# Operands of a gate made beside another block's out product, stored operands split later, attention outputs stored later

## The chip, the cores and the metric

The kernel runs on one core of a Trainium2 chip. A core has five engines with an instruction queue each: TensorE (PE, matrix products, with its weight loads shown apart as PEld), VectorE (DVE), ScalarE (ACT), GpSimd (POOL) and SyncE (SP). In this kernel SP does nothing but issue DMAs, and all DMAs are issued there, in the order of its queue: an issue that must wait (for a buffer, or for the data to be stored) holds back every issue behind it. The metric is the device time of one execution in microseconds; the time of a version is the median of its runs.

## The reference

One layer of a streaming encoder on 2048 prompt frames and 32 sample frames, in single precision, width 1024:

```
a  = rmsnorm(h) @ w_in                         # one projection, split into q, k, v of two groups
oa = differential attention                    # group A: 4 heads, two softmaxes each, v of 128
ob = chunk-band attention                      # group B: 8 heads of 64, a band of 9 chunks of 64
h  = h + concat(rmsnorm(oa), rmsnorm(ob)) @ w_out
c  = rmsnorm(h)
h  = h + square(relu(c @ w_up)) @ w_down       # 1024 -> 4096 -> 1024
h  = h + sigmoid(h @ w_ple_gate) * (p @ w_ple_proj)
y  = rmsnorm(h)
```

Beside `y` the new keys and values of both groups are outputs. Everything runs for the prompt and for the sample frames, which also see a cache of 128 older frames.

## The kernel before, in words

**Tiling.** The frames lie in four blocks: three of 512, and block 3 of 544 (512 prompt frames and the 32 sample frames). Activations are kept transposed, features on the 128 partitions, as eight tiles of 128 features. Every large product is made of three matmuls (`mm3`, lines 216 to 218): each operand is split into a rounded part and a rest (`split`: a copy on ACT, line 181, and a subtraction on POOL, lines 166 and 176, or on DVE, line 187), and high x high, high x low and low x high are summed in PSUM. Weights are loaded raw (`wr`, 512 KB each) and split in two halves (`piece`) by `wunit`; the pieces form a ring of a few units, which a unit leaves when TensorE has read it.

**Stages.** First the projections with the short attention (`attn_a` with `small`), then band attention, then the long attention of group A (`attn_a` for pairs 4 to 8) interleaved with the out products and MLPs of blocks 0 and 1, then block 1's gate. After that comes the part that most of the change touches, in `run`, lines 1595 to 1640:

- block 2's out product (`outproj(2)`), with the loading of block 3's attention outputs;
- block 3's out product, `outproj(3)`: eight groups `d` of 48 matmuls, which add to the residual (`hd`), square it on ACT and sum the squares on POOL (`sqacc`). Beside its last five groups runs `cparts(2)` in four steps `k`: each loads two tiles of block 2's residual (`tmp<-hS`), normalizes them (line 1011), and forms and splits the seven operands of block 2's MLP (`cs`; subtractions at lines 1023 to 1026);
- `h` of block 0 is loaded whole (2 MB, `h<-hS`) into memory that `outproj(3)`'s operands held, and `gate(0)` splits it into `hu` (eight ACT copies, four subtractions on DVE, four on POOL) and multiplies: eight groups of 24 matmuls `gps<-hu` and 6 of `pps<-pT`, a sigmoid on ACT, and an add into `h` on POOL (line 1361). Beside it, block 2's MLP makes its first weights;
- `mlp7(2)`: block 2's MLP, sixteen chunks, each with seven half-size up products (`ups`) and eight groups of down products (`dps`). Beside it run `final(0)`, four steps that write `y`, and `cstage(3)`, which prepares block 3's MLP operands as `cparts` does, but stores them to DRAM (`cst`, from rows `ct`) in eight steps: per `k` a step with two loads and three splits, and a step with four subtractions and four splits. Each split is stored at once;
- block 2's gate, block 3's MLP (which loads the stored operands into `cs`), and block 3's gate and final.

**Order.** The functions are generators; `weave` takes a step of one after each step of another, which sets the order of allocation and of priority. The framework then orders each engine's instructions by a simulated timeline and picks the buffers of the rings, and each engine runs its instructions strictly in that order. `tc.issue_after(x)` places an instruction behind `x`.

**Attention outputs.** `attn_a_pair` (line 591) handles a pair of 128-frame tiles of one head: scores, two softmaxes, transposes, value products over chunks of four key tiles (`v`, loaded chunk by chunk, two buffers), and a norm whose last instruction on DVE writes `os` (line 733). The store `oT<-os` is issued right there. `os` has two buffers.

## Time and profile before

| | us |
|---|---|
| median of 3 runs | 3171.91 (3171.86 to 3174.97) |
| the profiled execution | 3169.83 |
| its span, first to last instruction | 3168.0 |
| TensorE busy | 3014.8 (95%) |
| VectorE, ScalarE, GpSimd busy | 1900.8, 1880.1, 1837.4 |
| mean granted TensorE clock | 0.981 |

Times in the rows count from the start of the span. A group or timeline row names the line of the kernel, the engine, the operation, the tile written and the tiles read; brackets show how long the engine had been idle before and what ended that. A row of the waits names the waiting engine, line and tile, then what it waited for, the total in us, how often, and the longest. A row of the windows gives a stretch, its length, the busy time of PE, PEld, DVE, ACT and POOL (instructions in brackets), the granted clock (1.00 is full), the share of the DMA engines and GB/s. In a row of one tile's instructions the three numbers behind the count are the shortest, median and longest duration in ns, then the first and last start. Lines of helpers (166, 176, 181, 187, 216 to 218, 157 for every DMA) are told apart by their tiles.

### The profile page before, as it was taken

What the parts mean: (1) busy time and instruction counts of PE and PEld (TensorE: products, weight loads), DVE (VectorE), ACT (ScalarE), POOL (GpSimd) and SP (SyncE); (2) the same over time, 40 slices, a digit from 0 to 9 for tenths busy, and PEclk for the clock granted to TensorE, in tenths of its full rate; (3) what the DMA queues carried; (4) which work ended last, traced back from release to release, by engine and by line L of the source; (5) the groups of instructions that cost most, each with busy time, mean ns of one, the idle gap of its engine ahead of it and who ended that gap; (6) DMA issues with size and microseconds to landing.
All of it is one profiled execution on the core that took longest, in us unless ns stands there. A gap on an engine that the chain in (4) does not pass through costs nothing. (4 is left out here: it accounts for less than half of the span.)

```text
span 3168.0 us, 52770 instructions
## 1 busy us (share of the span) xinstructions
PE 3014.8 (95%) x17913; PEld 2656.2 (84%) x17913; DVE 1900.8 (60%) x4596; ACT 1880.1 (59%) x4166; POOL 1837.4 (58%) x2496
## 2 busy tenths in 40 slices
PE   8999898999999999999999999999799999999998
PEld 7787787899877787878788788878688888999998
DVE  5158774655465654676756656435667885576653
ACT  6257775766676664766666657444555455554545
POOL 2447455332346544655655555677777778767674
PEclk9999999999999999999999999999899999999999
DMA  8788758986788645555563543537433446333231
GB/s 274 247 243 245 205 185 233 262 229 194 219 243 245 194 125 151 154 148 153 171 182 117 143 116 108 169 106 234 134 120 120 157 134 228 122 105 110 87 115 56
DMA packets 522134, 537.17 MB, mean 170 GB/s; under 512 B 38620, under 2 KB 401440, under 8 KB 521864
## 3 DMA queue, kind: packets, MB, share of 16 engines
q1 hardware_dynamic: 521864, 533.80, 56.6%
q8 instruction: 142, 2.33, 0.3%
q14 instruction: 128, 1.05, 0.1%
HBM read 419.88 MB, written 117.75 MB: 170 GB/s over the span
## 5 line engine op out<-in xcount | busy, mean ns | idle before, releaser
L176 POOL TENSOR_TENSOR wl<-wr,wh 128x256 fp32r<-128x256 f32 x648 | 473.2, 763 | 351.6 <-ACT wh L181 321.6
L181 ACT ACTIVATE piece<-wr 128x512 fp32r<-128x512 f32 x406 | 246.4, 625 | 283.9 <-PE ups L217 108.5
L176 POOL TENSOR_TENSOR piece<-wr,piece 128x256 fp32r<-128x256 f32 x404 | 326.1, 834 | 103.2 <-ACT piece L181 93.8
L181 ACT ACTIVATE wh<-wr 128x1024 fp32r<-128x1024 f32 x228 | 241.0, 1058 | 184.6 <-PE qps L217 42.1
L166 POOL TENSOR_TENSOR wl<-wr,wh 128x256 fp32r<-128x256 f32 x264 | 199.0, 786 | 199.7 <-ACT wh L181 193.4
L218 PE MATMUL dps<-uh,piece 128*128 128x272 f32 (+1 forms) x768 | 248.1, 325 | 6.0 <-POOL piece L166 5.9
L216 PE MATMUL dps<-uh,piece 128*128 128x272 f32 (+1 forms) x768 | 247.0, 325 | 5.0 <-ACT piece L181 2.1
L166 POOL TENSOR_TENSOR piece<-wr,piece 128x256 fp32r<-128x256 f32 x280 | 232.5, 862 | 27.1 <-ACT piece L181 22.8
L217 PE MATMUL dps<-ul,piece 128*128 128x272 f32 (+1 forms) x768 | 248.0, 324 | 0.0
L216 PE MATMUL ups<-cs,piece 128*128 128x256 f32 (+1 forms) x864 | 246.7, 286 | 1.0 <-DVE r L1219 1.0
L217 PE MATMUL ups<-cs,piece 128*128 128x256 f32 (+1 forms) x864 | 245.9, 285 | 0.0
L218 PE MATMUL ups<-cs,piece 128*128 128x256 f32 (+1 forms) x864 | 245.9, 285 | 0.0
L216 PE MATMUL qps<-aH,wh 128*128 128x512 f32 (+1 forms) x640 | 231.5, 362 | 9.1 <-ACT kn L506 4.5
L218 PE MATMUL qps<-aH,wl 128*128 128x512 f32 (+1 forms) x640 | 229.8, 359 | 0.0
L217 PE MATMUL qps<-aL,wh 128*128 128x512 f32 (+1 forms) x640 | 229.0, 358 | 0.0
L1160 DVE TENSOR_TENSOR h<-h,dps 128x512 f32<-128x512 f32 x256 | 174.6, 682 | 80.6 <-PE dps L218 75.0
L1208 DVE TENSOR_TENSOR h<-h,dps 128x272 f32<-128x272 f32 (+1 forms) x384 | 189.5, 514 | 54.8 <-PE dps L218 53.9
L216 PE MATMUL dps<-uh,wh 128*128 128x512 f32 x512 | 209.5, 409 | 12.5 <-DVE h L1160 6.1
L216 PE MATMUL ups<-cH,wh 128*128 128x512 f32 x512 | 203.0, 397 | 5.5 <-DMA kbt<-kS 5.1
L633 PE MATMUL s<-ka,q 128*128 128x512 f32 (+3 forms) x768 | 187.8, 345 | 17.5 <-ACT e L647 7.0
L218 PE MATMUL dps<-uh,wl 128*128 128x512 f32 x512 | 203.1, 397 | 0.5 <-POOL wl L166 0.4
L217 PE MATMUL dps<-ul,wh 128*128 128x512 f32 x512 | 202.3, 395 | 0.0
(314 smaller groups left out, 9636.9 us busy)
## 6 DMA issues: line engine op xcount, KB each, us to landing
wr<-w_up SPq DMA_DIRECT2D x128, 512.0 KB, 3.9
wr<-w_down SPq DMA_DIRECT2D x128, 512.0 KB, 3.8
wr<-w_in SPq DMA_DIRECT2D x74, 512.0 KB, 5.4
q<-qS SPq DMA_DIRECT2D x128, 256.0 KB, 5.1
v<-vSa SPq DMA_DIRECT2D x64, 512.0 KB, 3.8
ka<-kS SPq DMA_DIRECT2D x32, 512.0 KB, 9.3
wr<-w_out SPq DMA_DIRECT2D x32, 512.0 KB, 4.4
wr<-w_ple_gate SPq DMA_DIRECT2D x32, 512.0 KB, 4.3
```

The lines of the kernel that those rows point to most:

```text
L166: nc.gpsimd.tensor_tensor(out[:, sl], a[:, sl], b[:, sl], op=op)
L176: nc.gpsimd.tensor_tensor(out[:, sl], a[:, sl], b[:, sl], op=op)
L181: nc.scalar.activation(hi, raw, AF.Copy)
L216: nc.tensor.matmul(ps, lh, rh, start=start and i == 0, stop=False)
L217: nc.tensor.matmul(ps, lh, rl, start=False, stop=False)
L218: nc.tensor.matmul(ps, ll, rh, start=False, stop=stop and i == n - 1)
L633: nc.tensor.matmul(s, q[:, m, hl, P * qi : P * qi + nr], kt[:, m, k0 - kb : k0 - kb + n], start=hl == 0, stop=hl == 1)
L1160: nc.vector.tensor_tensor(hv, hv, ps, op=ALU.add)
L1208: nc.vector.tensor_tensor(hv, hv, ps, op=ALU.add)
```

## The change

Three edits. (1) A new generator, `hparts`, loads block 0's residual in eight tiles (`hraw<-hS`, 256 KB each) and splits them into `hu`; its three steps are taken after the first three groups of `outproj(3)`. `gate(0)` gets these operands (`made`) and splits nothing; it still loads `h` for the add. `cparts(2)` takes two of its four steps beside `outproj(3)` and the other two beside `gate(0)`, ahead of the first weights of block 2's MLP. (2) `cstage`: the four splits that follow the subtractions are issued after the next `k`'s rows are loaded and normalized, and the three splits of a `k` one step after its rows; nine steps in place of eight. (3) In `attn_a_pair` the store of `os` is kept in `late`, and issued behind the load of the third chunk of `v` of the next pair, or at the latest at the end of the next pair; with `small` it is issued at once, as before.

```diff
@@ attn_a, attn_a_pair
+        late = []
...
-                self.attn_a_pair(g, j if j < 8 else None, kt if j < 8 else ks, ba, pool, ps_s, ps_t, ps_o)
+                self.attn_a_pair(g, j if j < 8 else None, kt if j < 8 else ks, ba, pool, ps_s, ps_t, ps_o, late)
+                if self.small:
+                    late.pop(0)()
+        while late:
+            late.pop(0)()
...
-                self.dma(
+                ins = self.dma(
                     v[:, :nch].rearrange("p k a b -> p k (a b)"),
...
+                if c0 == 8 and late:
+                    with self.tc.issue_after(ins.ins):
+                        late.pop(0)()
...
-        self.dma(self.oT[:, g, t0 : t0 + nq], os_)
+        while late:
+            late.pop(0)()
+        late.append(lambda: self.dma(self.oT[:, g, t0 : t0 + nq], os_))
@@ cstage
+        def parts(k, *which):
+            for x, raw in which:
+                t = up.tile([P, up.aw], F32R, tag="u", name="cst")[:, :n]
+                self.split(t[:, :m], t[:, m:], raw, "act", "dve")
+                self.dma(out[x][:, :, k], t.rearrange("p (i c) -> p i c", i=2))
+
+        late = ()
         for k in range(4):
...
+            parts(k - 1, *late)
+            yield
             (b11, b12), (b21, b22) = c
...
-            parts(("b11", "dve"), ("b21", "dve"), ("b22", "dve"))
-            yield
+            parts(k, ("b11", b11), ("b21", b21), ("b22", b22))
             nc.vector.tensor_tensor(b22, b22, b12, op=ALU.subtract)
...
-            parts(("t2", "dve"), ("t1", "dve"), ("t3", "dve"), ("t4", "dve"))
+            late = (("t2", b11), ("t1", b12), ("t3", b22), ("t4", b21))
             yield
+        parts(3, *late)
+        yield
@@ hparts, gate
+    def hparts(self, b, wk, up, out):
+        n, t0 = BN[b], 512 * b
+        hH, hL = [[up.tile([P, BLK], F32R, tag="u", name="hu")[:, :n] for k in range(8)] for _ in range(2)]
+        out.append((hH, hL))
+        for k in range(8):
+            raw = wk.tile([P, BLK], F32, tag="tmp", bufs=self.nt, name="hraw")[:, :n]
+            self.dma(raw, self.hS[:, k, t0 : t0 + n])
+            self.split(hH[k], hL[k], raw, "act", "dve" if k % 2 else "pool")
+            if k in (2, 5):
+                yield
...
-        for k in range(8):
-            self.split(hH[k], hL[k], h[:, k, :n], "act", "dve" if k % 2 else "pool")
+        if made is None:
+            for k in range(8):
+                self.split(hH[k], hL[k], h[:, k, :n], "act", "dve" if k % 2 else "pool")
@@ run
                 g = self.outproj(3, wk, oa[3], md, acc[3])
+                made = []
+                hp = self.hparts(0, wk, up, made)
                 for _ in range(3):
                     next(g)
+                    next(hp, None)
                 r2 = self.colnorm(acc[2][0], 2, 1.0 / D, wk, mm, "mm", None)
-                weave(g, self.cparts(2, wk, cs, ops, r2), 1)
+                c = self.cparts(2, wk, cs, ops, r2)
+                weave(g, islice(c, 2), 1)
...
-            g = self.gate(0, h, up, None, md, wk)
+            g = self.gate(0, h, up, None, md, wk, made[0])
...
-            weave(g, self.along(iter(range(3)), m), 1)
+            weave(g, self.along(c, m), 1)
```

More of the change, by code (lines that the diff above doesn't have):

```diff
@@ L2 @@
 from contextlib import ExitStack
-from itertools import chain
+from itertools import chain, islice
 import numpy as np
@@ L1045, in cstage @@
                 c.append((tmp[:, :m], tmp[:, m:]))
+            parts(k - 1, *late)
+            yield
             (b11, b12), (b21, b22) = c
-            raw = {"b11": b11, "b21": b21, "b22": b22, "t3": b22, "t1": b12, "t2": b11, "t4": b21}
-            def parts(*which):
-                for x, e in which:
-                    t = up.tile([P, up.aw], F32R, tag="u", name="cst")[:, :n]
-                    self.split(t[:, :m], t[:, m:], raw[x], "act", e)
-                    self.dma(out[x][:, :, k], t.rearrange("p (i c) -> p i c", i=2))
-            parts(("b11", "dve"), ("b21", "dve"), ("b22", "dve"))
-            yield
+            parts(k, ("b11", b11), ("b21", b21), ("b22", b22))
             nc.vector.tensor_tensor(b22, b22, b12, op=ALU.subtract)
@@ L1301, in gfin, with gate @@
         self.dma(self.gf, self.a["g_final"].unsqueeze(0).broadcast_to([P, D]))
[L1303 removed]
+    def hparts(self, b, wk, up, out):
[8 more added lines that the diff above has]
+                yield
+    def gate(self, b, h, up, act, md, wk=None, made=None):
         nc, a = self.nc, self.a
@@ L1310, in gate @@
                 self.dma(pT[i][k][:, :n], self.pS[:, i, k, t0 : t0 + n])
-        if wk is None and act.aw is None:
+        if made is not None:
+            hH, hL = made
+        elif wk is None and act.aw is None:
             hc = [act.tile([P, 4, 272], F32R, tag="cs", name="hc").rearrange("p a b -> p (a b)") for _ in range(8)]
```

5 lines of the change are left out of this document (2 added, 3 removed).

## The prediction

> **What bounds the kernel now.** First the page: TensorE is busy for 95% of the span, so only its idle time and its slow stretches can be won. Then the chain of waits of PE, longest first, and the busy time by stretch (columns: PE, weight load, DVE, ACT, POOL, then granted clock, DMA share, GB/s).
>
> ```profile
> span 3168.0 us, 52770 instructions
> PE 3014.8 (95%) x17913; PEld 2656.2 (84%) x17913; DVE 1900.8 (60%) x4596; ACT 1880.1 (59%) x4166; POOL 1837.4 (58%) x2496
> ...
> GB/s 274 247 243 245 205 185 233 262 229 194 219 243 245 194 125 151 154 148 153 171 182 117 143 116 108 169 106 234 134 120 120 157 134 228 122 105 110 87 115 56
> ...
> PE gps L216 <- ACT hu L181: 20.2, 1, 20.2
> PE o L719 <- ACT pH L712: 7.4, 4, 3.7
> ...
> 2180.00:2228.00 48.00, 48.00 (x383) 47.91 (x382) 24.74 (x38) 19.57 (x39) 38.15 (x49) 1.00 0.72 215
> 2228.00:2249.00 21.00, 0.76 (x7) 0.54 (x5) 20.17 (x32) 10.62 (x25) 15.40 (x19) 0.63 0.76 259
> 2249.00:2290.00 41.00, 41.00 (x167) 33.02 (x168) 14.88 (x18) 21.53 (x38) 32.96 (x42) 0.94 0.18 52
> ...
> 2450.00:2620.00 170.00, 164.39 (x1017) 145.56 (x1016) 137.38 (x209) 89.90 (x175) 134.72 (x151) 1.00 0.46 150
> 2740.00:3090.00 350.00, 349.01 (x2782) 348.69 (x2781) 239.45 (x480) 175.74 (x320) 250.68 (x316) 1.00 0.32 103
> ```
>
> One wait stands far above the rest: at the start of block 0's gate TensorE is idle for 20.2 us, waiting for `hu`, the gate's operands. In those 21 us VectorE is busy for 20.17: it is the bound there, and for nobody but the gate. The timeline shows why.
>
> ```profile
> 2228.36 0.28 PE L218 MATMUL ops<-oact,piece 128*128 128x272 f32 x1
> 2248.89 0.80 PE L216 MATMUL gps<-hu,piece 128*128 128x512 f32 x1 [20.24 <-ACT hu L181]
> ...
> 2253.75 0.45 PE L216 MATMUL pps<-pT,piece 128*128 128x512 f32 x1
> 2254.03 0.39 PE L217 MATMUL pps<-pT,piece 128*128 128x512 f32 x1
> ...
> 2256.12 0.39 PE L217 MATMUL gps<-hu,piece 128*128 128x512 f32 x1
> ...
> 2229.74 0.74 DVE L1011 SCALAR_TENSOR_TENSOR tmp<-tmp,g_mlp_s,r 128x512 f32<-128x512 f32 x1
> ...
> 2238.50 0.74 DVE L1011 SCALAR_TENSOR_TENSOR tmp<-tmp,g_mlp_s,r 128x512 f32<-128x512 f32 x1
> ...
> 2247.24 0.41 DVE L187 TENSOR_TENSOR cs<-tmp,cs 128x256 fp32r<-128x256 f32 x1
> ...
> 2248.22 4.26 ACT L181 ACTIVATE hu<-h 128x512 fp32r<-128x512 f32 x8
> ...
> 2235.99 0.57 SPq L157 DMA_DIRECT2D h<-hS  x1
> ```
>
> Block 3's out product ends at 2228.4. VectorE is then still in the last two of `cparts`' four steps: one starts at 2229.74, the next at 2238.50 (8.76 us a step), the last subtraction at 2247.24. ACT's `hu` copies stand behind them in ACT's order and start at 2248.22. After the idle time the first eleven matmuls, 2248.89 to 2253.75, are 4.86/11 = 0.442 us apart; from 2254.03 to 2256.12 nine steps take 0.232 each. So the stall costs 20.24 + 11 x (0.442 - 0.232) = 20.2 + 2.3 = 22.5 us. That is by far the largest single item of this trace.
>
> **The change, part by part.** *Gate operands earlier.* Eight loads `hraw` (256 KB each) and eight splits are issued with the first three groups of block 3's out product; `cparts` keeps two steps there, and its other two go beside the gate. In the changed program's order all eight ACT copies stand ahead of `cparts`' first one, so nothing of the late chain holds the gate. Gone: 20.2 + 2.3 us. What was added, and its cover:
>
> - DMA: 2 MB of `hraw`, and 1 MB of `pT` that was loaded before block 2's out product, in 48 us that moved 215 GB/s x 48 = 10.3 MB. Without the two `tmp` loads that leave this stretch (0.5 MB), 12.8 MB is 267 GB/s; the page's fastest slice moved 274. The share was 0.72, so I cost it at nothing; without that cover it would be 2.5 MB at 259 GB/s, 10 us, on weight loads that run several groups of 6 us ahead.
> - SP: eight issues more; `h<-hS` is still loaded (the residual add needs it) but only after the out product's last matmul, in whose memory it lies. Behind it on SP stand `w_up` twice, `cparts`' last four loads and three gate weights. The first reader of `h` is POOL's add of the gate's first group, with 19 POOL instructions ahead of it in the gate; the load takes 10.1 us (the landing row below).
> - ACT and DVE: the splits are moved, not added: 4.3 us of ACT, and of DVE the same four subtractions. Two steps of `cparts`, 17.5 us of DVE, go into a gate in which DVE was busy for 14.88 of 41: covered. They are due when block 2's MLP starts, 55.7 us after the gate does.
> - POOL is the engine to watch. The gate is 8 groups x 30 matmuls x 0.232 = 55.7 us of PE.
>
> ```profile
> L176 POOL TENSOR_TENSOR piece<-wr,piece 128x256 fp32r<-128x256 f32 x60 | 47.8, 824 | 10.7 <-ACT piece L181 10.3
> ...
> L166 POOL TENSOR_TENSOR hu<-h,hu 128x256 fp32r<-128x256 f32 x8 | 7.5, 971 | 0.3 <-ACT hu L181 0.3
> ...
> L166 POOL TENSOR_TENSOR hu<-h,hu x8: 736/1008/1181, 2248.9 to 2255.7; 128x256 fp32r<-128x256 f32 x8
> ...
> DMA to landing us min/median/max: 10.1/10.1/10.1
> ```
>
> In the out product POOL has 48 - 38.15 = 9.9 us free; `hu` takes 7.5 (8 x 0.971). From the gate's second weight on, POOL's order holds 59 instructions up to the last gate weight, and 39 up to the second half of the fifth group's. At 0.824 each that is 48.6 and 32.1 us from about 2228. The fifth group's half is due 4 x 6.96 us plus 14 matmuls, 31.1 us, after 2228.4; the last one 52.0 us after. So POOL is 0.6 us late at the fifth group and in time at the end: I take 1.0 us of new stall. The ends: none at 0.736 each; at 1.181 each 59 take 69.7 us, 17.3 too many. I take 0.824 because its row is of these very instructions, sixty of them in this stretch.
>
> The Trainium skill, "SBUF — State Buffer", section "SBUF: two separate sides", speaks against packing more of DVE beside POOL: it says that a two-input DVE operation and a POOL operation exclude each other on a shared port pair for a whole instruction. The spread from 736 to 1181 ns of one POOL form, the long ones beside DVE's own `hu` subtractions, agrees with it. By that rule alone the stall would be up to 17 us in place of 1; it is the first rival.
>
> *Stored operands split a chunk later (`cstage`).* Loads, splits and stores keep their number; the splits that follow a row load are issued one step later, so that no store waits at the head of SP for a load that has just been issued. There is one step more, nine instead of eight; with `final`'s four that makes 13 in a loop of 14.
>
> ```profile
> PE dps L218 <- POOL piece L166: 3.9, 6, 1.0
> PE dps L216 <- ACT piece L181: 1.5, 2, 1.1
> ...
> SPq L157 <- DVE cst L187: 10.9, 13, 1.7
> ...
> L187 DVE TENSOR_TENSOR cst<-ct,cst x28: 427/974/984, 2460.0 to 2615.5; 128x272 fp32r<-128x272 f32 x28
> ...
> L216 PE MATMUL gps<-hu,piece x128: 388/396/795, 2248.9 to 2720.7; 128*128 128x512 f32 x128
> ```
>
> While `cstage` runs (2450 to 2620) PE waits 5.4 us in eight waits, all for weights of the down product; SP waits 10.9 us for `cst`, and `w_down` stands behind it. At most 5.4 us can go. The third MLP runs a like loop without `cstage` for 350 us with 1.0 us of PE idle, but there each chunk has more PE time to hide in. I take 1.5 us, since most of the waits are for POOL, whose work does not change. The other end: the last stores come one chunk later (84 matmuls of half width and 48 of full width, 90 x 0.232 = 21 us), some 2637 in place of 2616, and what they hold is first read behind block 2's gate, whose last group is at 2720.7. So a loss has no room but in reordering; 1 us, the longest single wait here.
>
> *Attention outputs stored a pair later.* In the long attention stage (1120 to 2060) each `oT<-os` goes behind the third value load of the next pair; the short stage keeps its order. A pair's buffer is one of two and is wanted again two pairs on, so a store one pair late holds nobody. First the waits of that stage (SP, PE, ACT), then the two PE waits that follow a late load.
>
> ```profile
> SPq L157 <- DVE os L733: 54.1, 14, 11.8
> ...
> PE s L633 <- DMA q<-qS: 4.0, 4, 1.7
> ...
> ACT wh L181 <- DMA wr<-w_down: 29.4, 6, 9.0
> ...
> 1646.00 0.70 PE L633 MATMUL s<-ka,q 128*128 128x512 f32 x2 [0.87 <-DMA q<-qS]
> ...
> 1770.80 1.06 ACT L181 ACTIVATE wh<-wr 128x1024 fp32r<-128x1024 f32 x1 [7.50 <-DMA wr<-w_down]
> ...
> 1773.81 0.50 PE L216 MATMUL dps<-uh,wh 128*128 128x512 f32 x1 [2.98 <-ACT relu L1125]
> ```
>
> SP loses 54.1 us at the head of its queue, but PE waits for a load it delays only 4.0 us. Most of SP's time then goes to the next wait in line, a raw weight buffer. I take half of 4.0: 2.0 us. The ends: 4.0 + 2.98 = 7.0 gained; lost, 2.98 at one place if a burst of key loads that now starts earlier pushes a weight load back.
>
> *The sum* against the profiled execution's own 3169.83 us: - 20.2 - 2.3 + 1.0 - 1.5 - 2.0 = - 25.0, that is 3144.8. The median of the three runs shown is 3171.91, 2.1 above the profiled one; so 3147 for the median.
>
> **The rivals.**
> 1. *POOL becomes the bound in the gate.* DVE is busier beside it, each POOL instruction takes the 1.18 us that `hu` shows, and 17.3 us of the stall come back as waits for weights. For it: POOL had 32.96 of 41 us in the gate. Against: sixty like instructions took 0.824. 3171.9 - 22.5 + 17.3 - 3.5 = 3163.
> 2. *The stores free more than PE's waits show.* The whole 7.0 us and all 5.4 of `cstage`: 3171.9 - 22.5 - 12.4 = 3137. Against: few PE waits follow SP's.
> 3. *Slower: the stores' new place makes a weight load late at every pair.* Loads that no longer wait behind a store go out in one burst with the keys, and each of the 20 stores moved costs the 2.98 us that the late `w_down` at 1773.81 cost: 60 us, 3171.9 - 25 + 60 = 3207. It decides from nine pairs on (9 x 2.98 = 26.8). Against: ACT waited for a `w_down` six times in 940 us, 29.4 us together, and TensorE felt little of it.
> 4. *The change doesn't do what it says*: the `hu` splits land late and the gate waits as before, 3170. Against: they are issued with the first three of eight groups of 6 us (48 us in all), 30 us before they are due.
>
> **How the numbers follow.** Forecast 0.63 (3141 to 3153 by itself); rival 1 0.15; rival 2 0.10; rival 3 0.06; rival 4 0.06. The range 3136 to 3163 leaves out rivals 3 and 4 and the far ends of rivals 1 and 2. 0.2% is 6.3 us, about what a measurement of this kernel can tell: faster is the forecast, rival 2 and nearly all of rival 1, 0.87; same is rival 4 and the rest of rival 1, 0.07; slower is rival 3, 0.06.
>
> **What would show it.** In the profile after: no wait of `gps` for `hu`, granted clock near 1.00 where it was 0.63; `hu` splits of `hraw` before `cparts`; gate waits for POOL's pieces of about 1 us (17 says rival 1); waits for `cst` gone from SP and PE's waits in block 2's MLP below 5.4; `DVE os` gone from SP's waits in the long attention and `q<-qS` below 4.0. It is wrong if block 2's MLP starts with a wait for `cs`, or if ACT waits for `w_down` more often than in six places.

## The result, and the profile after

| | before | after |
|---|---|---|
| median of five executions (us) | 3171.91 (3169.77 to 3175.32) | 3156.93 (3146.42 to 3159.81) |
| ratio, 95% interval | | 0.9941, 0.9928 to 0.9954 |
| the profiled execution, its span | 3169.83, 3168.0 | 3146.42, 3144.6 |

The change makes the kernel 15 us faster by the medians, and 18.7 us (14.6 to 22.8) by the ratio, which is formed from all executions; 25 us, to 3147, was predicted. The measured median lies inside the stated range of 3136 to 3163, but 10 us above the forecast and only 6 us below the price of rival 1. The profiled execution of the changed kernel is the fastest of its five, so the two traces stand 23.4 us apart, and only a part of that is the change. The page of the changed kernel, and its waits of PE over the whole span (longest first, rows between left out):

```profile
span 3144.6 us, 52811 instructions
PE 3011.4 (96%) x17913; PEld 2649.6 (84%) x17913; DVE 1897.6 (60%) x4596; ACT 1878.1 (60%) x4166; POOL 1847.6 (59%) x2496
```

```profile
PE o L727 <- ACT pH L720: 7.8, 4, 3.7
...
PE gps L216 <- ACT piece L181: 6.5, 1, 6.5
...
PE s L638 <- DMA q<-qS: 3.6, 4, 1.6
```

The 20.2 us wait of `gps` for `hu` is gone. In its place stands a new wait of 6.5 us of the same product for a `piece`, a split gate weight. The busy time by stretch (PE, weight load, DVE, ACT, POOL, clock, DMA share, GB/s) for the last 48 us of block 3's out product, for the 21 us that were the stall, for 41 us of gate, and for `cstage` (here 175 us long), each shifted by what the changed kernel is ahead:

```profile
2170.00:2218.00 48.00, 48.00 (x381) 47.76 (x380) 21.34 (x33) 21.06 (x40) 40.17 (x51) 1.00 0.81 260
2218.00:2239.00 21.00, 19.55 (x85) 15.71 (x85) 12.33 (x20) 10.36 (x22) 19.00 (x24) 1.00 0.68 222
2239.00:2280.00 41.00, 32.87 (x132) 25.49 (x132) 31.34 (x42) 27.89 (x55) 37.24 (x43) 0.92 0.36 116
2425.00:2600.00 175.00, 172.10 (x1065) 152.55 (x1064) 145.10 (x219) 91.38 (x177) 144.41 (x158) 1.00 0.47 150
```

The out product carries the added loads and splits without losing anything (PE 48.00 of 48). The former stall is filled (19.55 of 21, full clock). But 8 us are lost in the gate behind it: TensorE is busy for 32.87 of 41 us where it was busy for all 41.00, at a clock of 0.92. The timeline of that place, PE, then SP, DVE and ACT:

```profile
2219.70 0.47 PE L216 MATMUL gps<-hu,piece 128*128 128x512 f32 x1 [1.45 <-DVE hd L980]
...
2250.24 0.50 PE L218 MATMUL gps<-hu,piece 128*128 128x512 f32 x1 [1.60 <-POOL piece L176]
...
2259.30 0.80 PE L216 MATMUL gps<-hu,piece 128*128 128x512 f32 x1 [6.46 <-ACT piece L181]
...
2233.63 8.29 SPq L157 DMA_DIRECT2D wr<-w_up  x2
2241.97 0.97 SPq L157 DMA_DIRECT2D tmp<-hS  x2
2246.69 0.38 SPq L157 DMA_DIRECT2D wr<-w_ple_gate  x1
2247.12 1.05 SPq L157 DMA_DIRECT2D tmp<-hS  x2
...
2246.58 0.74 DVE L1021 SCALAR_TENSOR_TENSOR tmp<-tmp,g_mlp_s,r 128x512 f32<-128x512 f32 x1
...
2254.58 0.42 ACT L181 ACTIVATE cs<-tmp 128x256 fp32r<-128x256 f32 x1 [1.41 <-DVE tmp L1033]
...
2258.31 0.42 ACT L181 ACTIVATE cs<-tmp 128x256 fp32r<-128x256 f32 x1 [1.31 <-DVE tmp L1035]
2258.63 0.62 ACT L181 ACTIVATE piece<-wr 128x512 fp32r<-128x512 f32 x1
```

The gate starts at 2219.70 after a wait of 1.45 us for the add (`hd`) of the out product's sixth group. Its fifth group stops twice, 1.60 us for POOL's half of a weight and 6.46 us for the second half on ACT, split at 2258.63, 38.9 us after the gate began. In front of that split ACT's order holds the `cs` copies of the two steps of `cparts` that the change moved here, and they wait for DVE. DVE begins the first of these steps at 2246.58. Its rows (`tmp<-hS`) were issued only at 2241.97, behind two `w_up` loads that held SP's queue for 8.29 us, and the first of them landed at 2245.95; in DVE's own order the step also stands behind work on the second `w_up`, for which DVE waited until 2245.37. After the wait eight matmuls are 0.43 us apart in place of 0.23: 1.6 us of slow clock.

Where the rest of the 23.4 us lies is told by the stages, measured between the same matmuls of both traces. Before the long attention, where neither kernel's order differs, the changed kernel is already 4.4 us ahead; at one place there TensorE waited 5.1 us for `kbt` in the execution of before and not in that of after. This is the comparison on which the experiments rest, so here are the stages of every kernel that was profiled (the other names are the experiments below), worked out from the starts of matmuls in its timeline. Each row is one execution, and they come from different chips (us; A: the long attention with the MLPs beside it, matmul 6300 to 11100; B: from there to the last matmul of block 3's out product; C: to the gate's first; D: to the gate's last, a `pps`; E: to block 2's gate; F: to the end of the last matmul):

```
                A      B     C     D      E      F    B+C+D against before
before        983.1  132.6  20.5  57.9  358.9  489.8     0.0
gate_only     982.8  132.7   1.8  66.5  359.3  490.4   -10.1
cst_only      984.0  132.5  20.6  57.5  355.3  491.3    -0.4
attn_only     977.7  132.5  21.1  57.3  358.4  490.4    -0.1
after         976.9  132.8   1.7  66.1  355.6  490.6   -10.4
after_again   981.8  133.2   1.1  67.3  357.0  490.6    -9.4
late2         980.0  133.7   1.8  65.2  356.7  491.1   -10.3
three         976.9  131.8   0.1  69.6  357.0  490.3    -9.4
all4          981.9  133.5   2.1  70.0  355.5  490.5    -5.4
early1        980.5  139.4   0.3  63.9  353.0  492.6    -7.4
early2        982.9  143.1   2.9  57.2  357.1  492.4    -7.7
pre1          976.7  137.7   4.4  64.6  356.2  491.4    -4.2
ladder_out    981.1  132.5   3.4  63.9  356.3  492.5   -11.2
ladder_gone   980.1  132.8   1.5  66.4  354.6  491.8   -10.4
```

### The profile page after: what moved, and what is told of

It is laid out like the page before. It is cut to its first block, busy times and chain, and to the rows that moved or that the text cites. A ratio compares the mean times of both kernels' runs of the same rounds, so it can differ in the third digit from the quotient of the medians.

```text
span 3144.6 us, 52811 instructions
## 1 busy us (share of the span) xinstructions
PE 3011.4 (96%) x17913; PEld 2649.6 (84%) x17913; DVE 1897.6 (60%) x4596; ACT 1878.1 (60%) x4166; POOL 1847.6 (59%) x2496
## 3 DMA queue, kind: packets, MB, share of 16 engines
q14 instruction: 129, 1.05, 0.1%
## 5 line engine op out<-in xcount | busy, mean ns | idle before, releaser
L166 POOL TENSOR_TENSOR piece<-wr,piece 128x256 fp32r<-128x256 f32 x280 | 237.0, 878 | 26.9 <-ACT piece L181 21.5
L217 PE MATMUL ups<-cL,wh 128*128 128x512 f32 x512 | 201.2, 393 | 0.0
```

The source lines that it names most:

```text
L166: nc.gpsimd.tensor_tensor(out[:, sl], a[:, sl], b[:, sl], op=op)
L217: nc.tensor.matmul(ps, lh, rl, start=False, stop=False)
```

## The experiments

Each median stands beside that of the kernel before, run on the same chip in the same series; a ratio is formed from all executions of both and has its 95% interval.

**attn_only: the late stores alone.** The changed `attn_a` and `attn_a_pair`; the rest as before.

```diff
...
+                if c0 == 8 and late:
+                    with self.tc.issue_after(ins.ins):
+                        late.pop(0)()
...
-        self.dma(self.oT[:, g, t0 : t0 + nq], os_)
+        while late:
+            late.pop(0)()
+        late.append(lambda: self.dma(self.oT[:, g, t0 : t0 + nq], os_))
```

> Only the attention part of the change: the long attention's outputs stored a pair later, gate and cstage as before. The prediction's step gave this -2.0 us. The traces of before and after stand 6.1 us nearer the end of the long attention than at its start (from 4.43 us ahead to 10.54 us ahead, between matmul 6300 and matmul 11100), and 4.4 us of the lead of after was there already at 1083 us, in front of the long attention, where neither kernel's order differs. Theory 1 (the stores' 2.0 us, the rest of that lead is chance of that execution): 3168 to 3171 us, profile 2 us shorter than before's between the first and the last pair. Theory 2 (the late stores free SP's queue of more than was priced, the rival with 7.0 + 5.4 us): 3164 to 3167 us, 5 to 7 us between those two points. Both: no wait of SP for DVE os left in the long attention.

Measured: 3165.31 against 3166.43, ratio 0.9994 (0.9985 to 1.0002). Stage A is 5.4 us shorter in its profile. But A varies: 976.7 to 982.9 in the eleven profiles with late stores, 982.8 to 984.0 in the three without; the means differ by 3.6. So the profiles put the part at some 3 to 4 us. Its own executions put it at 1.9 us by the ratio (from a loss of 0.6 to a gain of 4.7), which agrees with the 2.0 predicted and leaves out theory 2's 5 to 7; one profile can't tell the theories apart. The waits of SP for `os` over the whole span fell, but not to nothing as both theories had it:

```profile
SPq L157 <- DVE os L741: 24.4, 10, 3.8
```

Before they were 64.1 us, 54.1 of them in the long attention, with a longest of 11.8.

**cst_only: the later splits of the stored operands alone.**

```diff
...
+            parts(k - 1, *late)
+            yield
             (b11, b12), (b21, b22) = c
-            parts(("b11", "dve"), ("b21", "dve"), ("b22", "dve"))
-            yield
+            parts(k, ("b11", b11), ("b21", b21), ("b22", b22))
...
-            parts(("t2", "dve"), ("t1", "dve"), ("t3", "dve"), ("t4", "dve"))
+            late = (("t2", b11), ("t1", b12), ("t3", b22), ("t4", b21))
             yield
+        parts(3, *late)
+        yield
```

> Only the stored operands of block 3 are split a chunk behind their rows (cstage). Prediction's step: -1.5 us. The traces of before and after differ by 3.3 us between the start of block 2's MLP and the gate of block 2. Theory 1 (step priced right): 3170 to 3171 us. Theory 2 (the part is worth the whole 3.3 to 4.5 us seen in the two traces): 3167 to 3169 us. Rival: the gain in the MLP is given back at the gate of block 2, where the lead of after falls from 25.6 to 23.0 us: then 3171 to 3172 us.

Measured: 3165.34 against 3166.43, ratio 0.9993 (0.9982 to 1.0004), which by itself can't be told from no change. In its profile stage E is 3.6 us shorter and F 1.5 longer: 2.1 in all. Over all kernels E + F is 2.0 us shorter with this part than without it (ten profiles against three; 1.8 with `ladder_out` counted). So the profiles say about 2 us, a part of E's gain being given back behind block 2's gate, as the rival said.

**gate_only: the gate's operands and the two moved steps alone.**

```diff
...
+                hp = self.hparts(0, wk, up, made)
...
-                weave(g, self.cparts(2, wk, cs, ops, r2), 1)
+                c = self.cparts(2, wk, cs, ops, r2)
+                weave(g, islice(c, 2), 1)
...
-            weave(g, self.along(iter(range(3)), m), 1)
+            weave(g, self.along(c, m), 1)
```

> Only block 0's gate operands beside block 3's out product, with two of the four steps of cparts moved into the gate. Prediction's steps: -20.2 - 2.3 + 1.0 = -21.5 us. Trace of after: 20.2 us of waits for hu fall to 1.9, but the fifth group of the gate now waits 6.5 us for a weight piece on ACT and 1.6 us for one on POOL, and the lead of after grows by 10.5 us from the last group of the out product to block 2's MLP. Theory 1 (the fifth group's wait belongs to the move and gives back 8 us, and some clock): 3160 to 3163 us, with a wait of 6 to 9 us in the fifth group. Theory 2 (the fifth group's wait is an accident of one execution): 3150 to 3152 us, and no such wait.

Measured: 3159.28 against 3166.43, ratio 0.9978 (0.9968 to 0.9987), 7.0 us (4.1 to 10.1) where the prediction's steps had 21.5. Its waits of PE between 2180 and 2300:

```profile
PE gps L216 <- ACT piece L181: 6.5, 1, 6.5
PE gps L218 <- POOL piece L176: 1.6, 1, 1.6
PE gps L216 <- DVE hd L970: 1.5, 1, 1.5
```

The same three waits as in the changed kernel, to the tenth: they belong to this part, and of the 18.8 us that leave stage C, 8.6 come back in stage D. Theory 1 holds, and theory 2's 20 us are out of reach.

**all4: no step of `cparts` in the gate.**

```diff
-                weave(g, islice(c, 2), 1)
+                weave(g, c, 1)
...
-            weave(g, self.along(c, m), 1)
+            weave(g, self.along(iter(range(2)), m), 1)
```

> The changed kernel, but with all four steps of cparts beside block 3's out product as before, so that none lies in the gate. Theory 1 (the gate's fifth group waits 6.5 + 1.6 us because ACT, which takes its work in order, has the second half of that group's weight split behind the splits of the third and fourth step of cparts, which wait for DVE): without them in the gate the wait is under 1.5 us, the clock of 2249 to 2290 us goes back from 0.92 to 1.0, and the time is 8 to 10 us under the changed kernel's, 3147 to 3149 against its median of 3156.9. Theory 2 (the fifth group waits for its weight's load or for POOL's share, which the steps of cparts do not set): the wait stays within 2 us of 8.1 and the time within 2 us of the changed kernel's. Theory 3 (the steps were in the way of the gate's operands: DVE has 29 of 48 us busy beside the out product's end, two steps add some 15): the splits of hu come late, PE waits 5 to 12 us for them at the gate's start, and the time is at or above the changed kernel's.

Measured: 3157.42 against 3166.43, ratio 0.9967 (0.9955 to 0.9979). The gate is not shorter but longer, 70.0 us. Its waits:

```profile
PE gps L216 <- DVE sig L1370: 3.1, 1, 3.1
PE gps L216 <- DVE hd L980: 3.0, 2, 1.8
PE gps L216 <- ACT piece L181: 2.7, 1, 2.7
PE gps L216 <- ACT cs L181: 1.0, 1, 1.0
PE gps L218 <- POOL piece L176: 0.4, 1, 0.4
```

The wait for the weight falls to 2.7 + 0.4 us, but 7.1 us of waits for DVE's results and for `cs` take its place. None of the three theories had this. The steps may be placed beside the out product, but each step's rows are issued on SP behind the store of the group before it: the last two at 2227.6 and 2237.5 here, where the out product ended at 2224.9 (2225.2 and 2233.6 in the kernel before, where it ended at 2228.4). So with the steps at these groups half of `cparts` falls behind the out product; in the kernel before it was the stall that gave it the time.

**after_again: the changed kernel once more.**

> The changed kernel once more, without an edit, beside the kernel before. What it is to tell: the profiled execution of the first look was the fastest of five (3146.4 of 3146.4 to 3159.8), and 4.4 us of its lead over the execution of before stood already at 1083 us, where TensorE had waited 5.1 us for kbt in one and not in the other though both kernels have the same order there. Theory 1 (that lead is chance of the execution, the gain of the change is what its own stages show, 10.2 us in the gate and out product's end, 2 to 3 in cstage, 2 in the long attention): ratio 0.995 to 0.996 (3150 to 3153 us where before has 3166). Theory 2 (the change is worth the 23.4 us of the two profiled executions): ratio 0.9926, 3143 us. Both: again a wait of 6 to 9 us in the gate's fifth group.

Measured: 3153.82 against 3172.26, ratio 0.9941 (0.9928 to 0.9953): the ratio of the first series, between the two theories. Its profiled execution is 14.2 us shorter in span than that of before, and has the wait in the gate again:

```profile
PE gps L216 <- ACT piece L181: 7.9, 2, 7.6
```

The 4.4 us ahead of the long attention are chance on the side of before: the stretch with the `kbt` wait (matmul 6000 to 6300) took 66.9 us there, and 61.3 to 65.8 in all thirteen other profiles, none of which changes the order there.

**three, early2, late2: other places for the steps and for the MLP's first weights.** In `three`, three steps of `cparts` stand beside block 3's out product. In early2 all four do, the first of them two groups earlier, with block 2's norm moved up. In late2 two empty steps stand in front of `mlp7`'s first weights.

```diff
# three
-                weave(g, islice(c, 2), 1)
+                weave(g, islice(c, 3), 1)
# early2
...
-                for _ in range(3):
+                next(g)
+                next(hp)
+                r2 = self.colnorm(acc[2][0], 2, 1.0 / D, wk, mm, "mm", None)
+                c = self.cparts(2, wk, cs, ops, r2)
+                for _ in range(2):
                     next(g)
                     next(hp, None)
-                r2 = self.colnorm(acc[2][0], 2, 1.0 / D, wk, mm, "mm", None)
-                c = self.cparts(2, wk, cs, ops, r2)
-                weave(g, islice(c, 2), 1)
+                    next(c)
+                weave(g, c, 1)
...
-            weave(g, self.along(c, m), 1)
+            weave(g, self.along(iter(range(2)), m), 1)
# late2
-            weave(g, self.along(c, m), 1)
+            weave(g, self.along(chain(c, iter(range(2))), m), 1)
```

> The changed kernel with three steps of cparts beside block 3's out product and one beside the gate, in place of two and two. With all four beside the out product the weight waits of the gate's fifth group fell from 8.1 to 3.1 us, but waits for DVE (hd 3.0, sig 3.1) and cs (1.0) came in their place. Theory 1 (DVE's work of cparts, 35 us, is the bound of out product and gate together; DVE stood idle in 2230 to 2245 because the loads of the third step are issued behind two w_up loads that wait 8.3 us for a buffer): with the third step's loads issued earlier DVE has work in 2230 to 2245, the fifth group waits 2 to 5 us in place of 8.1, all waits of the gate together are 4 to 7 us against 9.6, and the time is 2 to 5 us under the changed kernel's of the same chip. Theory 2 (POOL's share of weights and leads, busy for 9.9 of 10 us in 2240 to 2260, is the bound): the waits stay at 9 to 10 us in all, the time within 2 us of the changed kernel's.

> The changed kernel with all four steps of cparts beside block 3's out product, and the first of them two groups earlier (after the out product's second group, the loads of a step in front of its residual load), so that none is left for the gate and none comes late. Theory 1 (DVE's chain of cparts is the bound, and it starts late because each step's loads stand on SP behind a store of the out product that waits for TensorE): DVE starts that chain some 12 us earlier, the gate's waits fall to 0 to 3 us in all from 9.6 (10.2 with four steps at the old places), the clock stays at 1.00, and the time is 6 to 10 us under the changed kernel's. Theory 2 (POOL is the bound of the gate): waits for POOL's pieces of 5 us or more stay, and the time is within 2 us. Theory 3 (the earlier loads crowd the out product's weights, DMA share 0.74 to 0.82 there): TensorE waits for pieces in the out product, 2 us or more, which it does not in the changed kernel.

> The changed kernel with the first weights of block 2's MLP taken two steps of the gate later (two empty steps between cparts' last step and mlp7's first). On SP two gate weights and the loads of cparts' third step then stand in front of the w_up loads. Theory 1 (the chain of cparts on DVE is late in the gate because its loads are late on SP, and the splits of w_up lie in the same stretch on DVE and POOL): the fifth group's waits fall from 8.1 to 0 to 4 us, time 3 to 7 us under the changed kernel's, if the weights are still ready when block 2's MLP starts; a wait for lead or piece at its start takes back as much as it is long. Theory 2 (ACT's order behind cparts alone counts, whatever else is there): fifth group's wait 6 us or more, time within 2 us.

Measured, against 3172.26: three 3161.28, ratio 0.9967 (0.9955 to 0.9979); early2 3163.63, 0.9973 (0.9963 to 0.9984); late2 3156.95, 0.9959 (0.9946 to 0.9971). None is faster than the changed kernel of the same series (3153.82). The waits of PE in out product and gate of early2:

```profile
PE css L1100 <- ACT sh L181: 4.2, 1, 4.2
PE gps L216 <- DVE hd L980: 2.7, 1, 2.7
PE ops L216 <- ACT cs L181: 2.5, 1, 2.5
```

In early2 the gate runs without a wait for a weight in 57.2 us, but the out product is 10.5 us longer. In three the weight waits are 3.2 on ACT and 3.0 on POOL, with 4.2 us for `hd` and `sig`: 10.4 in all, where theory 1 had 4 to 7. In late2 the wait for the weight stays at 6.4: on SP a second gate weight now stands in front of the rows and waits for a buffer for the same 8.29 us, so the rows come no earlier.

**early1, pre1: one group earlier; rows one step ahead.**

```diff
# early1: the norm behind the second group, the first step behind the third
-                for _ in range(3):
+                for _ in range(2):
                     next(g)
                     next(hp, None)
...
-                weave(g, islice(c, 2), 1)
+                next(g)
+                next(hp, None)
+                next(c)
+                weave(g, c, 1)
...
-            weave(g, self.along(c, m), 1)
+            weave(g, self.along(iter(range(2)), m), 1)
# pre1, in cparts: rows of k + 1 loaded in step k
...
+            for x in ((0, 1), (2,), (3,), ())[k]:
+                load(x)
             for i in range(2):
...
+                tmp = rows.pop(0)
...
```

> As the kernel with cparts' first step two groups earlier, but one group earlier only, with block 2's norm behind the out product's second group in place of its first. With two groups earlier the gate had no wait for a weight (57.4 us from its first matmul to block 2's MLP, against 66.4 in the changed kernel), but the out product lost 10.5 us: 4.2 because the norm's matmul stood in PE's order before its operand was there, 2.5 for cs on ACT, 2.7 for hd on DVE, the rest in slow clock. Theory 1 (the place of the norm is what cost the out product; DVE has room between 2150 and 2215): no wait for sh, out product 2 to 5 us longer than in the changed kernel, gate 57 to 60 us, time 3 to 6 us under the changed kernel's. Theory 2 (DVE is full from the out product to the gate, so work taken out of the gate comes back in front of it): the waits in out product and gate together are again 8 us or more, and the time is not under the changed kernel's.

> The changed kernel with the loads of cparts' rows issued one step ahead of their use (the third step's rows with the second step, beside the out product; the work on them stays beside the gate). What it is to tell: whether the gate's fifth group waits because the third step's rows come late (issued at 2242 to 2248 behind two w_up loads that wait 8.3 us for a buffer), or because that step's work lies in the gate at all. Theory 1 (late rows): DVE, busy for 9.2 of 20 us in 2230 to 2250, takes the third step there, the fifth group waits 0 to 3 us in place of 8, the time is 4 to 8 us under the changed kernel's. Theory 2 (the work itself, wherever its rows are): waits of 7 us or more stay, as DVE's or POOL's, and the time is within 3 us of the changed kernel's or above it, as with three steps beside the out product.

Measured, against 3168.64: early1 3153.77, ratio 0.9950 (0.9938 to 0.9963); pre1 3156.80, 0.9964 (0.9952 to 0.9976). Neither ratio is better than the changed kernel's 0.9941, and early1's can't be told from it. In both, out product and gate together are longer than in the changed kernel (7.4 and 4.2 us under before, against 10.4 and 9.4). In early1 the early norm's wait falls from 4.2 to 0.9 us, but 2.8 us for `cs` in the out product and 2.6 for a weight and 1.9 for `cs` in the gate remain. The waits of pre1:

```profile
PE gps L216 <- DVE hd L980: 4.1, 1, 4.1
PE gps L216 <- ACT piece L181: 3.7, 1, 3.7
PE ops L216 <- DVE hd L980: 3.4, 1, 3.4
```

The wait for the weight falls to 3.7, and DVE's adds come late instead, in the out product (3.4) and at the gate's start (4.1): DVE takes its work in order too, and the steps now stand in front of the adds that free PSUM. Theory 2 holds for both.

**ladder_out, ladder_gone: DVE's part of the two steps left out.** In the third and fourth step of `cparts` the subtractions on DVE are left out, those that form the operands and those that make low parts. In ladder_out copies on ACT write these low parts; in ladder_gone they are set to zero ahead, by five short instructions on DVE beside the out product. Half of block 2's MLP operands are then not what the layer needs: these two kernels tell only of time.

```diff
# ladder_out
...
+                    if k < 2 or e == "pool":
+                        self.split(ops[x][0][:, k], ops[x][1][:, k], raw[x], "act", e)
+                    else:
+                        nc.scalar.copy(ops[x][0][:, k], raw[x])
+                        nc.scalar.copy(ops[x][1][:, k], raw[x])
...
# ladder_gone
...
+                    if k == 0 and e == "dve":
+                        nc.vector.memset(ops[x][1][:, 2:].bitcast(F32), 0.0)
+                    if k < 2 or e == "pool":
+                        self.split(ops[x][0][:, k], ops[x][1][:, k], raw[x], "act", e)
+                    else:
+                        nc.scalar.activation(ops[x][0][:, k], raw[x], AF.Copy)
...
# both
...
-            nc.vector.tensor_tensor(b22, b22, b12, op=ALU.subtract)
...
+            if k < 2:
+                nc.vector.tensor_tensor(b22, b22, b12, op=ALU.subtract)
...
```

> The changed kernel without the part of cparts' third and fourth step that DVE does behind the normalizing: the four subtractions are left out, and the low parts that DVE subtracts are written by a copy on ACT instead, so that half of block 2's MLP operands are not the right ones; the loads, POOL's share and the number of ACT's copies ahead of each weight piece stay or grow (ten copies more on ACT in the two steps, of 0.4 us). Theory 1 (ACT, in order, waits for DVE's ladder of subtractions, and the second half of the fifth group's weight stands behind it): the 6 to 8 us wait for that piece falls to 0 to 3 us, the time is 5 to 9 us under the changed kernel's. Theory 2 (POOL's share, busy for 9.4 to 10 of 10 us in 2240 to 2260, or the weight's load sets the fifth group): the wait stays at 5 us or more, as a wait for POOL's piece or ACT's.

> The changed kernel without the part of cparts' third and fourth step that DVE does behind the normalizing, this time with nothing put in its place: the four subtractions and the ten low parts that DVE subtracts in these two steps are left out (that half of the low parts is set to zero at cparts' first step, five short instructions on DVE beside the out product), so that half of block 2's MLP operands are not the right ones. Loads, POOL's share and ACT's copies in these two steps stay as in the changed kernel; some 11 us of DVE's work in 2250 to 2275 are gone. In the version with copies on ACT in the place of DVE's subtractions the fifth group still waited 4.5 us, with ten copies of 0.32 us more in front of the piece: 4.5 - 3.2 = 1.3 us is what should be left without them. Theory 1 (ACT, in order, stands behind DVE's work, and the second half of the fifth group's weight behind ACT): the wait for that piece is 0 to 2 us, against 6.5 and 7.6 in the changed kernel's two profiles, and the time is 5 to 9 us under the changed kernel's, a ratio of 0.991 to 0.993 to before. Theory 2 (POOL's share or the weight's load sets that group): the wait stays at 4 us or more.

Measured: ladder_out 3153.22 against 3168.64, ratio 0.9947 (0.9936 to 0.9959), a wait of 4.5 us for the piece, between the two theories and blurred by its own copies; ladder_gone 3156.76 against 3170.50, ratio 0.9957 (0.9943 to 0.9971). The timeline of ladder_gone there, SP and ACT, and its busy time in the 10 us around:

```profile
2252.53 0.97 SPq L157 DMA_DIRECT2D tmp<-hS  x2
...
2257.63 1.05 SPq L157 DMA_DIRECT2D tmp<-hS  x2
...
2263.11 0.61 ACT L181 ACTIVATE piece<-wr 128x512 fp32r<-128x512 f32 x1
...
2265.74 1.63 ACT L1035 ACTIVATE cs<-tmp 128x256 fp32r<-128x256 f32 x5
2267.27 0.40 ACT L181 ACTIVATE cs<-tmp 128x256 fp32r<-128x256 f32 x1
2267.58 0.62 ACT L181 ACTIVATE piece<-wr 128x512 fp32r<-128x512 f32 x1
```

```profile
2260.00:2270.00 10.00, 5.89 (x14) 4.41 (x15) 6.69 (x8) 8.27 (x21) 10.00 (x13) 0.70 0.18 62
```

Theory 1 as it was put fell: with DVE's subtractions gone, the split that TensorE waits for comes 37.9 us after the gate's first matmul (2229.7) in place of 38.9. The wait itself is shorter, 3.9 us, but the matmuls before it run at half clock, and out product and gate together are exactly as in the changed kernel (10.4 under before). The rows are as late as there (22.9 and 28.0 us after the gate's start, against 22.3 and 27.4), the split still stands behind them and their `cs` copies in ACT's order, and POOL is busy for all of the 10 us around it (fifth busy time of the window's row). In both traces the split follows the `cs` copy in front of it at once (2258.31 and 2258.63 there, 2267.27 and 2267.58 here), so ACT's order is what it comes last behind; in the changed kernel that order stands behind DVE, here behind the late rows and ACT's own copies. Whether late rows, ACT's order or POOL's holds the fifth group is not told apart: every version that eased one met another.

## Why the prediction was right, and where it was wrong

**The stall, - 20.2 and - 2.3.** Right in mechanism and nearly in size. Stage C falls from 20.5 to 1.7 us (1.1 in the repeat); what remains is the wait for the add of the out product's sixth group, `hd`, which the prediction did not name. The gate's first matmuls run at full clock.

**The new stall, + 1.0: the step that failed.** The place was right, the gate's fifth group, and the size was off by a factor of ten. The gate took 57.9 us before, 2.3 of it slow clock; it takes 66.1 and 67.3 now, so 10.5 to 11.7 are lost in it (8.1 and 8.4 of waits, the rest slow clock and steps between). Three readings led there; a fourth, of POOL's order, stands under rival 1. "Two steps of `cparts`, 17.5 us of DVE, go into a gate in which DVE was busy for 14.88 of 41: covered" took an average over 41 us and asked when the `cs` operands are due (55.7 us), not what stands behind them in ACT's order: the gate's own weights do, due 31.1 us in. The SP line named the queue ("`w_up` twice, `cparts`' last four loads and three gate weights") and did not price the wait of the second `w_up` for a buffer, 8.29 us. And the stall was counted as lost time, though it was in that time that half of `cparts` was done; in none of the five other places tried for it, all4, three, early1, early2 and pre1, was there room for this work between out product and gate: each takes off one wait and meets another. With this the part is worth 10 us by the stages (- 10.4, - 9.4, and - 10.1 alone) in place of 21.5, and 7.0 (4.1 to 10.1) by the executions of gate_only.

**Rival 1, POOL the bound in the gate, 17.3 us back.** About half of its price came back, and TensorE's wait is named for POOL in 1.6 us of it. POOL's pieces did not take 1.18 us each: from 2228 to 2290 they took

```profile
L176 POOL TENSOR_TENSOR piece<-wr,piece 128x256 fp32r<-128x256 f32 x32 | 26.1, 842 | 3.5 <-ACT piece L181 3.5
L166 POOL TENSOR_TENSOR piece<-wr,piece 128x256 fp32r<-128x256 f32 x4 | 3.9, 996 | 0.0
```

close to the 0.824 that was taken. But POOL was busy for 19.00 of 21 us and 37.24 of 41, so it has no room. The prediction's 39 instructions are the right count: they run from the second weight's first half, at 2225.42, to the fifth group's second half. They are not all pieces, though, and take 0.894 us each, 34.9 in all; and they begin 5.7 us after the gate where the prediction had them begin with it. So they end at 2260.94, 41.2 us after the gate's start, where 31.1 was due. The last of them:

```profile
2254.23 1.77 POOL L166 TENSOR_TENSOR h<-h,sig 128x256 f32<-128x256 f32 x2
2255.96 2.04 POOL L176 TENSOR_TENSOR piece<-wr,piece 128x256 fp32r<-128x256 f32 x2
2257.96 0.90 POOL L166 TENSOR_TENSOR cs<-tmp,cs 128x256 fp32r<-128x256 f32 x1
2259.33 1.61 POOL L176 TENSOR_TENSOR piece<-wr,piece 128x256 fp32r<-128x256 f32 x2 [0.47 <-ACT piece L181]
```

In front of the last low part POOL stands idle for 0.47 us (0.47 in gate_only too, 1.32 in the repeat), and before that not at all since 2240.07. In this order of POOL's work an earlier split on ACT would thus have brought that low part only about half a microsecond sooner: POOL is nearly as late as ACT, and rival 1 was nearer to the mechanism than its price for one instruction. The sharing shows on DVE as well, whose 128 x 256 subtractions here have a shortest of 409 ns and a median of 942:

```profile
L187 DVE TENSOR_TENSOR cs<-tmp,cs x18: 409/942/962, 2216.8 to 2267.6; 128x256 fp32r<-128x256 f32 x18
```

The Trainium skill, "SBUF — State Buffer", section "SBUF: two separate sides", says that a DVE operation with two inputs and a GpSimd operation lock each other out for whole instructions and that whoever is late waits; these durations agree, with DVE as the one that waits more.

**DMA, SP, ACT in the out product, at nothing.** Right: 260 GB/s moved in those 48 us where 267 was worked out, TensorE at 48.00 of 48.

**Stored operands, - 1.5.** Measured 2.0 over the profiles. The sign and size held in the profiles, the reason did not: SP's waits for `cst` were to go and rose, from 10.9 us in 13 waits to 21.2 in 27 over the whole span.

```profile
SPq L157 <- DVE cst L187: 21.2, 27, 4.8
```

What fell are TensorE's waits for weights of the down product in that stage, from 5.4 to 2.7 us, and some of that is given back in stage F. The waits of the changed kernel there:

```profile
PE dps L216 <- ACT piece L181: 2.7, 5, 1.3
```

Gone are just the waits for POOL that the prediction held to be beyond reach: 3.9 to 4.5 us in the three profiles without this part, at most 0.2 in the eleven with it. What in the order does this was not tried.

**Attention outputs, - 2.0.** Measured 3.6 in the mean of the profiles, between 0 and 6 in single ones, and 1.9 by the executions of attn_only. `DVE os` is not gone from SP's waits in the long attention but falls from 54.1 to 15.2 us:

```profile
SPq L157 <- DVE os L741: 15.2, 5, 3.8
```

The wait for `q<-qS` hardly moved (4.0 to 3.6); the single largest gain is the one that the upper end of that step named, the 2.98 us at 1773.81 behind a late `w_down`, which is not there in the trace of after. The waits of ACT for `w_down` are six still, 25.3 us. Rival 3's bursts did not come, and block 2's MLP starts without a wait for `cs`, the other sign of being wrong that the prediction named.

**The sum.** From the stages: - 10.0 (the mean of - 10.4, - 9.4 and - 10.1) - 2.0 - 3.6 = - 15.6, against 15.0 and 18.4 by the medians of the two series and 18.7 by both ratios, where - 25.0 was predicted. The parts measured alone add up to less, 7.0 + 2.2 + 1.9 = 11.1 us by their ratios. Whether the parts help each other or the chips differ stays open: the repeat of the whole ran on another chip than the parts. That the first profiled execution, 3146.42, stands within 2 us of the 3144.8 of the sum is a coincidence: it holds the 4.4 us of chance ahead of the long attention and a long attention at the short end of its range.

## What to carry to other kernels

Before a stall is counted as gain, list what the other engines do during it: work that was done in its shelter has to go somewhere. Here DVE, POOL and the loads were near full on both sides, and about half of the stall came back as several small waits. When work is moved beside a stage, the question is not whether an engine has room on the average of that stage, nor when the moved work is due, but what stands behind it in each in-order queue (ACT's copies, SP's loads) and when that is due. A gain of ten microseconds in a kernel whose executions vary by as much is read stage by stage, between the same instructions of several profiles, not from one pair of traces.

## What was not expected of the hardware

Executions of one program vary by 13.6 us (3161.07 to 3174.64 in 28 of the kernel before on one chip). One part of it goes with the time that loads take to land: a stretch whose order no version changes took 61.3 to 66.9 us, and three loads of 256 KB in it took 11.5 us in the median from issue to landing in the profile of before and 8.3 in that of after.

The clock can fall without a long idle time. In ladder_gone two waits of 0.61 and 1.05 us, 2 us apart, were followed by eight matmuls 0.43 us apart; in the changed kernel a wait of 1.60 us at the same place was followed by one step of 0.34 and then by steps of 0.23 to 0.24. The rows of ladder_gone:

```profile
2258.41 0.50 PE L216 MATMUL gps<-hu,piece 128*128 128x512 f32 x1 [0.61 <-ACT piece L181]
...
2260.20 0.56 PE L218 MATMUL gps<-hu,piece 128*128 128x512 f32 x1 [1.05 <-POOL piece L176]
2260.56 0.63 PE L216 MATMUL gps<-hu,piece 128*128 128x512 f32 x1
2260.98 0.63 PE L217 MATMUL gps<-hu,piece 128*128 128x512 f32 x1
```

The traces' own record of the clock tells the two cases apart. In each of the fourteen traces every change of the clock lies on a grid of 3.41 us. In ladder_gone both waits fell into one step of that grid, 2257.07 to 2260.49, in which TensorE was busy for 1.76 of 3.42 us, and the clock was halved at its end. In the changed kernel an edge of the grid, 2249.20, lay inside the wait, and the two steps were busy for 2.79 and 2.38 us. Over all fourteen traces the clock fell after 192 of the 193 full-clock steps that were busy for under 0.45 of their length (by the matmul ends of the traces), and after 6 of the 11961 that were busy for over 0.65.

The Trainium skill, "TensorE: Matmul & The Clock Gate", section "What's actually happening", has the clock halved after an idle window of about 3.4 us; here a step that was half idle was enough, so the measurement goes further than that rule. The slow spell after the 6.46 us wait lasted eight matmuls, 3.5 us, which agrees with the 3.4 us that the same page of the Trainium skill gives for getting back to full speed; after the 20.24 us wait of before it was eleven matmuls, 4.9 us.
